# RMSNorm with every row written twice: one VectorE copy of two rows becomes two copies of one row

## The chip, the cores and the metric

The kernel runs on one core of a Trainium2 chip. The metric is the device time of one execution in microseconds (us). The kernel before took 238.42 us, the median of three runs that lie between 238.42 and 239.19 us.

The engines that matter here are ScalarE (ACT in the profile), VectorE (DVE), GpSimd (POOL), SyncE (SP, which issues the transfers of `x` and of the output), and the core's 16 DMA engines, which carry the transfers. TensorE (PE) computes nothing here.

## The reference

`x` is 8 x 512 rows of 2048 float32 numbers, `gamma` is one row of 2048. Each row is divided by its root mean square and multiplied by `gamma`, and every result row stands twice in the output, one directly after the other:

```
x_rep  = np.repeat(x, 2, axis=1)                       # (8, 1024, 2048)
rms    = np.sqrt((x_rep ** 2).mean(axis=-1, keepdims=True) + 1e-6)
out    = (x_rep / rms * gamma[None, None, :]).astype(np.float32)
```

So 33.55 MB are read and 67.11 MB are written. The work on a row is done once; the second output row is a copy.

## The kernel before, in words

**Tiling.** The 4096 rows are cut into four loads. One load (`load`, L50) brings eight consecutive rows to each of the 128 partitions: 128 x 16384 float32, 8.39 MB. Each load makes two stores (`store`, L53): four input rows of a partition, scaled and doubled, are eight output rows, again 128 x 16384 float32 and 8.39 MB. There are four loads and eight stores of the same size.

**Memory.** All of it passes through one buffer `y` in SBUF with 24 rows for each partition, named in three blocks of eight: `first` (rows 0 to 7), `second` (8 to 15), `third` (16 to 23). A load's data sit in rows 4 to 11 or in rows 16 to 23. A block of eight rows that is ready to store holds result rows at even places and their copies at odd places.

**Order.** The order is written by hand (L84 turns the automatic scheduling off), so each engine does its instructions in the order in which `four` lists them, and semaphores make one engine wait for another. `four(n, ...)` handles two loads and their four stores; it is called twice, as the two groups of the title. In one group:

1. SP issues both loads.
2. First tile (rows 4 to 7 of `y`): `squares` (ScalarE, L63, a sum of squares for each row, then the root at L67) and `scale` (VectorE, the reciprocal at L73, then for each row one multiplication by the reciprocal and by `gamma` at L75). `repeat` (L82) copies rows: two on ScalarE, two on VectorE. Store 0.
3. Second tile (rows 8 to 11 of `y`, L100 to L103): the four rows are scaled from the last to the first and spread out to rows 14, 12, 10 and 8. ScalarE then copies the two upper ones (to rows 15 and 13), VectorE the two lower ones (from 8 to 9 and from 10 to 11). Store 1 follows at L103. **The change is in VectorE's copy here.**
4. Third and fourth tile (from the second load): L104 takes the squares of both, then both are scaled and copied, and all these copies are ScalarE's. Store 2 is from block `first`, store 3 from block `third`.

**Waits around the change.** VectorE's copy at L102 stands behind the four multiplications of its tile on the same engine. Store 1 on SP waits for that copy and for ScalarE's copy at L101. VectorE's next instruction after the copy is the reciprocal of the third tile, which waits for ScalarE's root. The multiplications after it write into block `first`, so they wait until store 0 has landed. On SP, store 2 stands behind store 1 and waits for ScalarE's copies at L106 and L107. The loads of the second group stand behind store 3 and wait for stores of the first group to land, since they write over the same rows.

`gamma` is brought in once at the start, over ACT's DMA queue, and spread to all partitions by GpSimd (L131, L135).

Of the kernel before, what the change touches and what calls it, by code (L numbers as in the profile page):

```python
# [1 line left out]

# [4 lines left out]


@with_exitstack
def kernel(  # L10
    ctx: ExitStack,
    tc: tile.TileContext,
    x: bass.AP,
    gamma: bass.AP,
    out: bass.AP,
):
    nc = tc.nc
    P = nc.NUM_PARTITIONS
    f32 = mybir.dt.float32
    Act = mybir.ActivationFunctionType  # L20
    Alu = mybir.AluOpType

    B, S, D = x.shape
    Bo, So, Do = out.shape
    R = So // S
    assert R == 2 and D == Do and B == Bo and So == S * R
    eps = 1e-6
    inv_d = 1.0 / float(D)


    K = 4
    N = B * S
    ntiles = N // (P * K)
    assert N % (P * K) == 0 and ntiles == 8
    H = 2
    x_t = x.rearrange("b s d -> (b s) d").rearrange("(n p k) d -> n p k d", p=P, k=H * K)
    out_t = out.rearrange("b s d -> (b s) d").rearrange("(n p h j) d -> n h p (j d)", p=P, h=H, j=K * R)

    singles = ctx.enter_context(tc.tile_pool(name="singles", bufs=1))
    rows = ctx.enter_context(tc.tile_pool(name="rows", bufs=1))  # L40
    junk = ctx.enter_context(tc.tile_pool(name="junk", bufs=1, space=bass.MemoryType.PSUM))
    small = ctx.enter_context(tc.tile_pool(name="small", bufs=4))

    y = rows.tile([P, 3 * K * R, D], f32, name="y")
    first, second, third = 0, K * R, 2 * K * R

    def load(n, at):
        nc.sync.dma_start(out=y[:, at : at + H * K, :], in_=x_t[n])  # L50

    def store(n, h, to):
        nc.sync.dma_start(  # L53
            out=out_t[n, h], in_=y[:, to : to + K * R, :].rearrange("p j d -> p (j d)")
        )

    def squares(at, rows):

        n = len(rows)
        ss = small.tile([P, n], f32, name=f"ss{n}")  # L60
        for c, k in enumerate(rows):
            sq = junk.tile([P, D], f32, name="sq")
            nc.scalar.activation(  # L63
                out=sq[:], in_=y[:, at + k, :], func=Act.Square, accum_out=ss[:, c : c + 1]
            )
        rms = small.tile([P, n], f32, name=f"rms{n}")
        nc.scalar.activation(out=rms[:], in_=ss[:], func=Act.Sqrt, scale=inv_d, bias=eps_t[:])  # L67
        return rms

    def scale(at, to, rows, rms):  # L70
        n = len(rows)
        rstd = small.tile([P, n], f32, name=f"rstd{n}")
        nc.vector.reciprocal(out=rstd[:], in_=rms[:])  # L73
        for c, k in enumerate(rows):
            nc.vector.scalar_tensor_tensor(  # L75
                out=y[:, to + R * k, :], in0=y[:, at + k, :], scalar=rstd[:, c : c + 1],
                in1=gamma_b[:], op0=Alu.mult, op1=Alu.mult,
            )

    def repeat(to, k0, k1, copy):  # L80
        y_r = y[:, to + R * k0 : to + R * k1, :].rearrange("p (k r) d -> p k r d", r=R)
        copy(out=y_r[:, :, 1, :], in_=y_r[:, :, 0, :])  # L82

    ctx.enter_context(tc.manual_schedule())  # L84

    half = K // 2
    up, down = list(range(K)), list(range(K - 1, -1, -1))

    def four(n, constants):


        load(n, first + K)
        constants()
        load(n + 1, third)
        for rows in (up[:half], up[half:]):
            scale(first + K, first, rows, squares(first + K, rows))
        repeat(first, 0, half, nc.scalar.copy)
        repeat(first, half, K, nc.vector.tensor_copy)
        store(n, 0, first)
        scale(second, second, down, squares(second, down))  # L100
        repeat(second, half, K, nc.scalar.copy)  # L101
        repeat(second, 0, half, nc.vector.tensor_copy)  # L102
        store(n, 1, second)  # L103
        roots = [squares(third + h * K, up) for h in range(H)]  # L104
        scale(third, first, up, roots[0])
        repeat(first, 0, half, nc.scalar.copy)  # L106
        repeat(first, half, K, nc.scalar.copy)  # L107
        store(n + 1, 0, first)
        scale(third + K, third, up, roots[1])
        repeat(third, 0, K, nc.scalar.copy)  # L110
        store(n + 1, 1, third)

    gamma_b = singles.tile([P, D], f32, name="gamma_b")
    G, E = 16, 3
    C = D // G - E
    gamma_s = y[0:1, 0:2, :].rearrange("p k (c d) -> p (k c) d", c=G // 2)
    gamma_t = y[0:1, 2, :]
    eps_t = singles.tile([P, 1], f32, name="eps_t")

    def constants():  # L120
        nc.scalar.dma_start(
            out=gamma_s[0:1, :, :C],
            in_=gamma[: G * C].rearrange("(p c d) -> p c d", p=1, c=G),
        )
        for c in range(E):
            at = G * C + c * G
            nc.scalar.dma_start(
                out=gamma_t[0:1, c * G : (c + 1) * G],
                in_=gamma[at : at + G].partition_broadcast(1),
            )  # L130
        nc.gpsimd.partition_broadcast(  # L131
            out_ap=gamma_b[:, : G * C].rearrange("p (c d) -> p c d", c=G),
            in_ap=gamma_s[0:1, :, :C],
        )
        nc.gpsimd.partition_broadcast(out_ap=gamma_b[:, G * C :], in_ap=gamma_t[0:1, : E * G])  # L135
        nc.vector.memset(eps_t, eps)  # L136

        root = singles.tile([P, 1], f32, name="root")[:]
        nc.scalar.activation(out=root, in_=eps_t[:], func=Act.Sqrt)  # L139

    four(0, constants)
    four(2, lambda: None)


# [1 line left out]
_INS = ['x', 'gamma']  # L146
_OUTS = [((8, 1024, 2048), 'float32')]


# [23 lines left out]
```

## Time and profile before

| What | Before |
|---|---|
| median of three runs | 238.42 us |
| the profiled execution, its own time | 238.52 us |
| span of the profiled execution | 236.3 us |
| DVE busy | 84.4 us (36%), 47 instructions |
| ACT busy | 110.2 us (47%), 86 instructions |
| POOL busy | 2.8 us (1%) |
| packets of the transfers of `x` and the output | 98.7% of 16 engines' span |
| bytes moved | 100.68 MB, 426 GB/s over the span |
| VectorE copies of 128x4096 | 4, 2.294 us each |

The span runs from the first to the last recorded event; the execution's own time is 2.2 us longer. A busy time is the sum of an engine's instructions and says nothing on whether anyone waited for them. In a row of instruction groups, "L82 DVE COPY y<-y 128x4096" is line 82 of the kernel, engine VectorE, a copy inside the buffer `y` of 4096 elements in each of 128 partitions. In a row of the timeline, the first two numbers are the start and the duration in us, and the bracket at the end says how long the engine had been idle before it and what ended that idle time. SPq is SP's sequencer, which issues transfers.

### The profile page before, as it was taken

How to read it: one execution, taken by the hardware profiler on the slowest of the kernel's cores; microseconds unless marked ns; L12 is line 12 of the kernel's file. 1: busy time of each engine (PE TensorE's matmuls, PEld its weight loads, DVE VectorE, ACT ScalarE, POOL GpSimd, SP SyncE). 2: the span in 40 equal slices, each digit the busy share in tenths (PEclk: the TensorE clock that was granted, in tenths of full speed). 3: DMA queues.
4: the chain of work that ended last, by engine and by line, in shares of the span. 5: the costliest groups of instructions: out<-in, count | busy, mean ns of one | idle time of the engine just before them, and what ended most of it. 6: DMA issues, size and time to landing. Idle time of an engine off the chain costs nothing.

```text
span 236.3 us, 225 instructions
## 1 busy us (share of the span) xinstructions
DVE 84.4 (36%) x47; ACT 110.2 (47%) x86; POOL 2.8 (1%) x6
## 2 busy tenths in 40 slices
DVE  0000396594699500000000007929919992000000
ACT  2001989479998470000000049991999957400000
POOL 0110000000000000000000000000000000000000
DMA  9898989989898989999898988989898988989894
GB/s 355 356 532 355 521 366 466 422 388 499 355 532 356 521 366 466 422 399 488 355 532 355 510 377 377 510 355 532 355 532 355 510 377 388 499 355 532 355 532 177
DMA packets 1767, 100.68 MB, mean 426 GB/s; under 512 B 230, under 2 KB 230, under 8 KB 230
## 3 DMA queue, kind: packets, MB, share of 16 engines
q1 hardware_dynamic: 1728, 100.66, 98.7%
q10 hardware_dynamic: 38, 0.01, 0.0%
q14 instruction: 1, 0.01, 0.0%
HBM read 33.56 MB, written 67.11 MB: 426 GB/s over the span
## 4 chain that ended last, share of the span: by engine, by line
DMA 45%; ACT 26%; DVE 12%; issue 2%; DVEq 0%
DMA y<-in_x_dram 26%; DMA out_dram<-y 19%; ACT sq L63 15%; DVE y L75 12%; ACT y L82 11%; ACT rms L67 1%; DVE rstd L73 0%; DVEq L75 0%
## 5 line engine op out<-in xcount | busy, mean ns | idle before, releaser
L63 ACT ACTIVATE sq<-y 128x2048 f32<-128x2048 f32 x32 | 60.1, 1878 | 71.1 <-DMA y<-in_x_dram 70.4
L75 DVE SCALAR_TENSOR_TENSOR y<-y,rstd,gamma_b 128x2048 f32<-128x2048 f32 x32 | 73.8, 2348 | 1.6 <-DMA out_dram<-y 1.0
L82 ACT COPY y<-y 128x4096 f32<-128x4096 f32 (+1 forms) x10 | 42.6, 4283 | 19.1 <-DVE y L75 18.3
L73 DVE RECIPROCAL rstd<-rms 128x4 f32<-128x4 f32 (+1 forms) x10 | 1.7, 170 | 109.2 <-ACT rms L67 109.2
L82 DVE COPY y<-y 128x4096 f32<-128x4096 f32 x4 | 9.2, 2294 | 0.1
L63 ACT ACTIVATION_READ_ACCUMULATOR sq<-y 128x1 f32 x32 | 6.0, 186 | 0.0
L67 ACT ACTIVATE rms<-ss,eps_t 128x4 f32<-128x4 f32 (+1 forms) x10 | 3.0, 297 | 0.3
L139 ACT ACT_TABLE_LOAD x1 | 1.3, 1283 | 2.6 <-issue 2.6
L131 POOL PARTITION_BROADCAST gamma_b<-y x1 | 2.2, 2243 | 10.2 <-DMA y<-in_gamma_dram 10.2
L135 POOL PARTITION_BROADCAST gamma_b<-y x1 | 0.3, 323 | 10.2 <-DMA y<-in_gamma_dram 10.2
L136 DVE MEMSET eps_t<- 128x1 f32 x1 | 0.1, 59 | 0.8 <-PEq L157 0.8
L139 ACT ACTIVATE root<-eps_t 128x1 f32<-128x1 f32 x1 | 0.2, 202 | 0.0
L157 POOL MEMSET const-bfloat16-1.0<- 128x1 bf16 x1 | 0.1, 101 | 0.0
L157 POOL MEMSET const-uint8-127<- 128x1 uint8 x1 | 0.1, 101 | 0.0
L157 POOL MEMSET const-float32-0.0<- 128x1 f32 x1 | 0.1, 98 | 0.2 <-issue 0.2
L157 POOL MEMSET const-float32-1.0<- 128x1 f32 x1 | 0.1, 99 | 0.0
## 6 DMA issues: line engine op xcount, KB each, us to landing
out_dram<-y SPq DMA_DIRECT2D x8, 24.7
y<-in_x_dram SPq DMA_DIRECT2D x4, 31.4
y<-in_gamma_dram ACTq DMA_DIRECT2D x3, 0.1 KB
y<-in_gamma_dram ACTq DMA_DIRECT2D x1, 7.8 KB, 9.9
```

The costliest lines, as they stand in the source:

```text
L63: nc.scalar.activation(out=sq[:], in_=y[:, at + k, :], func=Act.Square, accum_out=ss[:, c : c + 1])
L67: nc.scalar.activation(out=rms[:], in_=ss[:], func=Act.Sqrt, scale=inv_d, bias=eps_t[:])
L73: nc.vector.reciprocal(out=rstd[:], in_=rms[:])
L75: nc.vector.scalar_tensor_tensor(out=y[:, to + R * k, :], in0=y[:, at + k, :], scalar=rstd[:, c : c + 1], in1=gamma_b[:], op0=Alu.mult, op ...
L82: copy(out=y_r[:, :, 1, :], in_=y_r[:, :, 0, :])
L131: nc.gpsimd.partition_broadcast(out_ap=gamma_b[:, : G * C].rearrange("p (c d) -> p c d", c=G), in_ap=gamma_s[0:1, :, :C],)
L135: nc.gpsimd.partition_broadcast(out_ap=gamma_b[:, G * C :], in_ap=gamma_t[0:1, : E * G])
L136: nc.vector.memset(eps_t, eps)
L139: nc.scalar.activation(out=root, in_=eps_t[:], func=Act.Sqrt)
L157: nc = _bacc.Bacc("TRN2", target_bir_lowering=False, num_devices=1)
```

## The change

In `four`, which runs once for each group, VectorE's copy of rows 8 and 10 of the buffer to rows 9 and 11 as one instruction of 128 x 2 x 2048 elements is written as two instructions of 128 x 2048 elements: first row 8 to 9, then row 10 to 11. Nothing else in the code changes; the lines behind it move down by one.

```
         scale(second, second, down, squares(second, down))
         repeat(second, half, K, nc.scalar.copy)
-        repeat(second, 0, half, nc.vector.tensor_copy)
+        for k in range(half):
+            repeat(second, k, k + 1, nc.vector.tensor_copy)
         store(n, 1, second)
```

Here `half` is 2 and `K` is 4.

## The prediction, made before the changed kernel ran

> **What bounds the kernel now.** I read the queues first, because the kernel does little arithmetic on each byte. The page's part on DMA queues:
>
> ```profile
> q1 hardware_dynamic: 1728, 100.66, 98.7%
> HBM read 33.56 MB, written 67.11 MB: 426 GB/s over the span
> ```
>
> Queue 1 holds the four loads and eight stores. Its packets take 98.7% of what 16 DMA engines have in the span, so hardly any time is left in which no transfer runs. VectorE (36%) and ScalarE (47%) are mostly idle.
>
> Next the chain of waits, for the moments at which transfers land:
>
> ```profile
> 0.72 21.98 DMA y<-in_x_dram
> ...
> 76.20 23.79 DMA out_dram<-y
> ...
> 100.00 38.79 DMA y<-in_x_dram
> ...
> 155.26 22.28 DMA out_dram<-y
> ```
>
> Load 0 lands at 22.70, store 2 of the first group at 99.99, the second group's first load at 138.79, its store 0 at 177.54. In their order in the queue these are transfers 1, 5, 7 and 9. So four transfers take 77.29 us (19.32 each), the next two 38.80 (19.40 each), the next two 38.75 (19.38 each). Three remain: 3 x 19.35 = 58.05 brings the last landing to 235.6, and the span ends at 236.3. The twelve transfers run end to end at one pace. Load 0 took 21.98, about 2.6 more than the pace; that is the start of an empty queue.
>
> Last I read the timeline around the copy, in both groups, with SP's issues:
>
> ```profile
> 44.26 9.26 DVE L75 SCALAR_TENSOR_TENSOR y<-y,rstd,gamma_b 128x2048 f32<-128x2048 f32 x4
> 48.91 3.60 ACT L82 COPY y<-y 128x4096 f32<-128x4096 f32 x1 [4.89 <-DVE y L75]
> 53.56 2.29 DVE L82 COPY y<-y 128x4096 f32<-128x4096 f32 x1
> 55.94 0.34 SPq L53 DMA_DIRECT2D out_dram<-y  x1
> 60.88 0.18 DVE L73 RECIPROCAL rstd<-rms 128x4 f32<-128x4 f32 x1 [5.03 <-ACT rms L67]
> 61.48 9.14 DVE L75 SCALAR_TENSOR_TENSOR y<-y,rstd,gamma_b 128x2048 f32<-128x2048 f32 x4 [0.42 <-DMA out_dram<-y]
> ...
> 169.54 2.29 DVE L82 COPY y<-y 128x4096 f32<-128x4096 f32 x1
> 171.91 0.34 SPq L53 DMA_DIRECT2D out_dram<-y  x1
> 176.86 0.18 DVE L73 RECIPROCAL rstd<-rms 128x4 f32<-128x4 f32 x1 [5.03 <-ACT rms L67]
> ```
>
> Three things are to be seen. The copy does end last before store 1: ScalarE's half ends at 48.91 + 3.60 = 52.51, VectorE's at 53.56 + 2.29 = 55.85, and SP issues 0.09 later. But the transfer ahead of it is still running: store 0, on which the multiplication at 61.48 waits, has landed by about 61.4 (22.70 + 2 x 19.35 = 61.40). So store 1 is issued 5.46 us before the queue needs it; in the second group 177.54 - 171.91 = 5.63 us. And VectorE itself idles 5.03 us after the copy, until ScalarE's root is there.
>
> **The change part by part.**
>
> *Removed:* two VectorE copies of 128x4096, one in each group, from the row
>
> ```profile
> L82 DVE COPY y<-y 128x4096 f32<-128x4096 f32 x4 | 9.2, 2294 | 0.1
> ```
>
> *Added:* four copies of 128x2048. The trace has no VectorE copy of that shape, so I bound a pair of them. From below, half of the long copy each: 2 x 1.147 = 2.294, an extra of 0. Less than that would need the step from one row to the next inside the long copy to cost something; ScalarE's copies speak against it, since four rows (7.018 us) take less than twice the time of two rows (3.599 us). The difference, 2 x 3.599 - 7.018 = 0.18, is what one more start costs on that engine. On VectorE the reciprocals of 2 and 4 elements take 162 and 175 ns on average, nearly all of it the fixed part of an instruction; behind each other, instructions overlap a little: four multiplications of 2.348 take 9.26, so they start (9.26 - 2.348) / 3 = 2.304 apart, an overlap of 0.044. I take 0.175 - 0.044 = 0.13 us more for a pair, because this row is of the same engine. The far end is that a one-row copy lost the pace of the long one (4096 elements in 2.294 us) and went at the pace of the multiplication: 2 x 2.348 = 4.70, or 2.40 more. So the extra is between 0 and 2.40 us for each group, and 0.13 is what I take.
>
> *Moved:* nothing. Put side by side, the instruction lists of the two kernels differ on VectorE alone, by the split. SP's twelve transfers keep their order and what they wait for, ScalarE's 58 instructions too. The second short copy carries no wait of its own. POOL has done its last work by 23.4 us, over 30 us ahead of the first split copy.
>
> *Added wait:* none, but store 1 now starts after the second copy: 56.07 in place of 55.94, and 172.04 in place of 171.91. Behind store 1 on SP stands store 2, issued at 76.20 after ScalarE's copies; behind the copy on VectorE stands the reciprocal, whose idle time shrinks from 5.03 to 4.90. Nobody else waits for this copy.
>
> *The cover:* store 1 must be in the queue before store 0 lands, and earlier by what a transfer needs to get going. In the stretches of the first microseconds, the load issued at 0.72 moves nothing before 1.50:
>
> ```profile
> 0.72:1.50 0.78, 0.06 (x1) 0.00 (x0) 0.00 (x0) 1.00 0.00 0
> 1.50:3.00 1.50, 0.00 (x0) 0.41 (x1) 0.00 (x0) 1.00 2.02 699
> ```
>
> So the lead is at least 0.78 us, and at most the 2.6 us that load 0 took over the pace. Even with the 2.6, the pair may grow by 5.46 - 2.6 = 2.86 us in the first group and by 3.03 in the second before the queue runs dry. The 0.13 is a twentieth of that, and the far end of 2.40 still fits. Were the cover gone, two groups would cost 2 x 0.13 = 0.26 us.
>
> *Sum:* 238.52 (the profiled execution: its span of 236.3 and 2.2 around it) + 0 = 238.5 us. That execution stands 0.10 above the median of the runs, 238.42, inside their spread of 0.77.
>
> [...]
>
> **The rivals.**
>
> *A, the extra start is exposed or something gets in between the two copies (slower).* Place: VectorE between the short copies. Price: one us of total time for each us by which a pair grows beyond the cover, 2.86 and 3.03 us by the careful reading. To be slower by 0.5% (1.2 us, which is about what a measurement of this kernel can tell from no change) the two groups must together exceed their cover by 1.2 us, that is grow by about 3.5 us each. Two copies at the multiplication's pace grow 2.40 and don't reach it. A pair that grew by 4 us would give 238.5 + 1.14 + 0.97 = 240.6. Nothing on VectorE in the trace shows a gap of this kind between instructions without a wait: the copy follows the multiplication within 0.04 us.
>
> *B, the transfers change pace (either sign).* Stretches between issues that wait on landings give the spread of one transfer: 100.00 to 119.61 is 19.61, 119.61 to 138.79 is 19.18. If all twelve went at 19.6, the time would be 12 x 0.25 = 3.0 us longer (241.5), at 19.2 it would be 1.8 us shorter (236.7). It decides from 0.1 us for each transfer on. For it: the transfers are the bound, so any change in them counts in full. Against it: those two stretches hold no VectorE and no ScalarE work at all, and they average 19.40, the same as the 19.32 and 19.38 of the stretches full of copies. A copy of the same bytes cut in two has no way to show there.
>
> *C, the copy was on the path and gets quicker (faster).* Were two short copies quicker than the long one and the path through them bare, the gain would be at most the whole copy in both groups, 2 x 2.29 = 4.6 us, to 233.9. Against it stands the queue at 98.7%: it is already full when store 1 arrives, 5.46 us early.
>
> *D, the change doesn't do what it says.* The lists of instructions show two copies of 128x2048 in place of one, in both groups, so this is out; merged again, the time would be 238.5 as well.
>
> **How the numbers follow.** No change, by the cover: 0.89. Rival A 0.02, since a pair would have to take over twice its time. Rival B 0.07, split 0.04 slower and 0.03 faster, for what a trace of one execution can't exclude. Rival C 0.02. So faster by over 0.5% is 0.05, within 0.5% is 0.89, slower 0.06. The range is that of the first case: the unknown cost of the pair adds nothing up to 2.40 us, so it rests on the spread of the runs, 0.77 us, taken about once to either side of 238.5 and a little more for rival B: 237.6 to 239.4. A wider range would only add rivals of 0.11 together.
>
> **What would show each step.** Right: four copies of 128x2048 with a mean between 1.15 and 1.3 us; VectorE idle about 4.9 us after the pair; store 1 issued near 56.1 and 172.0; queue 1 again above 98%; store 0 of the second group landing near 177.5; span near 236.3. Wrong on the copy's price: a mean near 2.35 us, with the time unchanged all the same. Wrong on the cover: a lower share of queue 1 and a gap in the transfers behind store 0. Wrong by rival B: store 1 issued in time, the queue full, and the landings still drift from the 19.35 pace.

## The result

The changed kernel took 238.20 us, the median of 21 runs (238.13 to 238.82), against 238.62 us for 21 runs of the kernel before (238.40 to 239.22). The ratio is 0.9987 with a 95% interval of 0.9981 to 0.9992. That is 0.13% faster, 0.3 to 0.4 us. It lies inside the predicted range, and inside the 0.5% that the text called no change; but the interval does not hold 1, so the predicted difference of nothing was wrong by these 0.3 us. Where they come from is the question of the experiments.

The profiled execution took 238.17 us, its span 236.2. On the page of the changed kernel, the queue of the loads and stores:

```profile
q1 hardware_dynamic: 1728, 100.66, 98.7%
```

and in its groups of instructions, kept apart by shape, VectorE's copies:

```profile
L82 DVE COPY y<-y 128x2048 f32<-128x2048 f32 x4 | 4.7, 1223 | 0.1
L82 DVE COPY y<-y 128x4096 f32<-128x4096 f32 x2 | 4.6, 2294 | 0.1
```

The queue is as full as before. A short copy takes 1.223 us, half of the long one and 0.076 more.

The timeline of the changed kernel around the pair, in both groups:

```profile
53.48 2.36 DVE L82 COPY y<-y 128x2048 f32<-128x2048 f32 x2
55.92 0.34 SPq L53 DMA_DIRECT2D out_dram<-y  x1
60.80 0.18 DVE L73 RECIPROCAL rstd<-rms 128x4 f32<-128x4 f32 x1 [4.96 <-ACT rms L67]
61.42 9.14 DVE L75 SCALAR_TENSOR_TENSOR y<-y,rstd,gamma_b 128x2048 f32<-128x2048 f32 x4 [0.44 <-DMA out_dram<-y]
...
169.54 2.36 DVE L82 COPY y<-y 128x2048 f32<-128x2048 f32 x2
171.98 0.34 SPq L53 DMA_DIRECT2D out_dram<-y  x1
176.87 0.18 DVE L73 RECIPROCAL rstd<-rms 128x4 f32<-128x4 f32 x1 [4.96 <-ACT rms L67]
```

The pair takes 2.36 us where the one copy took 2.29. Store 1 of the second group is issued at 171.98 in place of 171.91, and VectorE waits 4.96 us behind the pair where it had waited 5.03. And the chain of waits, for the landings:

```profile
0.72 21.89 DMA y<-in_x_dram
...
76.13 23.81 DMA out_dram<-y
...
99.95 38.83 DMA y<-in_x_dram
...
155.26 22.19 DMA out_dram<-y
```

Load 0 lands at 22.61, 0.09 us earlier than before; this is 30 us ahead of the first split copy. From there on the landings stand at 99.94, 138.78 and 177.45: 77.33, 38.84 and 38.67 us apart, before 77.29, 38.80 and 38.75. Nothing got faster at the place of the change.

So the profile shows no gain inside the work. It shows one elsewhere. The time of an execution is its span and a rest around it. In the two profiles the time fell by 0.35 us (238.52 to 238.17), the span by 0.13 (236.324 to 236.191), and the rest by 0.22, from 2.20 to 1.98. In all 21 runs of the changed kernel the rest is between 1.92 and 2.02, with a mean of 1.96. (The span of a run is on record to 0.1 us only, so a single rest is good to 0.05; the means are better.) It scatters far less than the span, so it is the figure to follow.

### The profile page after: what moved, and what is told of

Same layout as the page of the kernel before. It is cut to its first block, busy times and chain, and to the rows that moved or that the text cites. A ratio compares the mean times of both kernels' runs of the same rounds, so it can differ in the third digit from the quotient of the medians.

```text
span 236.2 us, 227 instructions
## 1 busy us (share of the span) xinstructions
DVE 84.6 (36%) x49; ACT 110.2 (47%) x86; POOL 2.8 (1%) x6
## 3 DMA queue, kind: packets, MB, share of 16 engines
q1 hardware_dynamic: 1728, 100.66, 98.7%
## 4 chain that ended last, share of the span: by engine, by line
DMA 45%; ACT 26%; DVE 12%; issue 2%; DVEq 0%
DMA y<-in_x_dram 26%; DMA out_dram<-y 19%; ACT sq L63 15%; DVE y L75 12%; ACT y L82 11%; ACT rms L67 1%; DVE rstd L73 0%; DVEq L75 0%
## 5 line engine op out<-in xcount | busy, mean ns | idle before, releaser
L82 DVE COPY y<-y 128x2048 f32<-128x2048 f32 (+1 forms) x6 | 9.3, 1580 | 0.1
```

## The experiments

Three theories stood against each other at first: "the split" (two short copies help by themselves), "chance" (two timings of one kernel may differ by 0.1%), and "length of the program" (two more VectorE instructions shorten the rest, whatever they do). "Around the span" in the expectations is the rest: time less span, taken for every run and averaged.

### One kernel twice, and the change once more

e1 is the kernel before, unchanged; e2 is the changed kernel.

> The kernel before, unchanged, timed as if it were a change: it shows how far two timings of one and the same kernel stand apart here. Theory 'the split' (the 0.13% comes from cutting the copy in two): a ratio of 1.000, with an interval that holds 1, within 0.05%; span about 236.3 us and about 2.2 us around it. Theory 'chance' (the 0.13% is what two timings of one kernel may differ by): a ratio that lies 0.1% or more from 1, or an interval that does not hold 1.

> The changed kernel once more. Theory 'the split': ratio about 0.9987 again, that is 0.3 us less. Theory 'chance': a ratio between 0.999 and 1.001. Both expect two short copies of 1.22 us each, store 1 issued near 56.0 and 171.9 us, and no gap in the transfers.

Measured, e1: ratio 0.9995 (0.9986 to 1.0004), rest 2.21 us over 11 runs. The 33 runs of the kernel before beside it have a rest of 2.20, between 2.15 and 2.24. Measured, e2: ratio 0.9984 (0.9971 to 0.9997), rest 1.96 over 11 runs, between 1.92 and 2.01. So the rests of the two kernels don't overlap in any run, while their spans do: 236.2 to 237.9 in the 33 runs of before, 236.2 to 236.7 in e2. Of the difference of the means (238.37 against 238.69, 0.32 us) the rest holds 0.25, and the 0.08 of the spans is small against their scatter: the spans of e1 lie 0.11 below those of the same kernel beside it. Chance falls for the rest.

### The same number of instructions, nothing split

```
         repeat(second, 0, half, nc.vector.tensor_copy)
+        nc.vector.memset(pad[:, n // 2 : n // 2 + 1], 0.0)
```

> The long copy stays in one piece, and VectorE gets two instructions more in all, one memset of 128x1 (about 59 ns) behind the copy of the second tile in each group. The program is as many instructions longer as the changed kernel, but nothing is split. Theory 'length of the program' (what gets shorter is outside the work, in the start or the end of the execution, because the program has two more VectorE instructions): ratio about 0.9987, and the time around the span falls from about 2.2 to about 2.0 us. Theory 'the split': ratio 1.000, since the copy is whole. Theory 'chance': a ratio anywhere within 0.1% of 1.

Measured: ratio 0.9992 (0.9983 to 1.0001), rest 1.96 us over 11 runs (1.92 to 2.01). The copy is whole in its timeline:

```profile
53.49 2.29 DVE L82 COPY y<-y 128x4096 f32<-128x4096 f32 x1
55.73 0.06 DVE L103 MEMSET pad<- 128x1 f32 x1
60.81 0.18 DVE L73 RECIPROCAL rstd<-rms 128x4 f32<-128x4 f32 x1 [5.02 <-ACT rms L67]
```

A memset of 0.06 us in idle time does to the rest exactly what the split does. The theory "the split" falls for this part of the gain: it isn't the copies that make the rest shorter. The whole time is 0.27 us lower in the mean, but its interval still holds 1, so here the rest shows the effect and the total alone would not.

### The split at another place

```
-        repeat(first, half, K, nc.vector.tensor_copy)
+        for k in range(half, K):
+            repeat(first, k, k + 1, nc.vector.tensor_copy)
```

> The same split, but of VectorE's copy of the first tile (ahead of store 0) in both groups; that of the second tile stays whole. The pair takes 2 x 1.22 less the overlap, about 0.07 us more than the whole copy, and store 0 is issued about 0.07 us later, near 39.3 us, 2 us before the load ahead of it has landed. Theory 'length of the program': ratio about 0.9987, as for the changed kernel. Theory 'the split': about 0.9987 only if a split helps wherever it is, else 1.000 or up to 0.14 us more. Theory 'chance': within 0.1% of 1 with no order.

Measured: ratio 0.9996 (0.9986 to 1.0005), rest 1.98 us over 11 runs (1.92 to 2.03), span 236.56 on average. Store 0 is issued at 39.23 in place of 39.24. The rest is that of the changed kernel again; the total is not separable from no change, because this kernel's spans came out 0.07 us above those of before.

### Which engine, and how many

e5 adds `nc.scalar.copy(out=pad[...], in_=eps_t[:])`, a copy of 128x1, behind ScalarE's copy in each group. e6 has the memset in the first group alone. e7 has four memsets in each group.

> Two instructions more in all, but on ScalarE: one copy of 128x1 behind its copy of the second tile in each group, about 0.2 us each. VectorE is as before. Theory 'VectorE's program' (the time around the span depends on how many instructions VectorE has): 2.20 us around the span, as before. Theory 'any longer program': 1.96 us, as in the changed kernel. Both: the span stays near 236.4 us, since the transfers are queued 4 us and more ahead.

> One VectorE instruction more: a memset of 128x1 in the first group alone. Theory 'VectorE's program, by the instruction': half the effect, about 2.08 us around the span. Theory 'VectorE's program, by a step': either 2.20 or 1.96 us, nothing between.

> Eight VectorE instructions more, four memsets of 128x1 in each group (4 x 0.06 us in idle time). Theory 'by the instruction', 0.12 us for each: 2.20 - 8 x 0.12 = 1.24 us around the span, if it goes on so far; theory 'by a step': 1.96 us again, or a value near 2.2 if the pattern returns. The span stays near 236.4 us in either case.

Measured: e5 has a rest of 2.21 us, as before; the ratio is 0.9997 (0.9982 to 1.0011). So two instructions more count on VectorE and not on ScalarE. e6, with one instruction, has a rest of 1.84 us (1.80 to 1.88) and a ratio of 0.9988 (0.9976 to 1.0001): in the rest this is more than two instructions gain, so neither "half the effect" nor "2.20 or 1.96" holds. e7 has 1.78 (1.74 to 1.81): not the 1.24 of a gain by the instruction. Its span however is 236.7 to 236.8 in all ten runs, and the total is that of before (ratio 0.9995, 0.9982 to 1.0009).

The next candidate for what orders these values is the transfer of the program itself: the page lists a queue of the kind "instruction", q14. In the kernel before and in the changed one the row says that one such transfer falls into the span. In e7 the row is

```profile
q14 instruction: 2, 0.02, 0.0%
```

The first of e7's two is the one at 75 us that every kernel here has. In the packet records behind the page there is, besides six ahead of the span, a second transfer of 8192 bytes like the first, in every kernel but e12. In e7 it starts at 191.3 us. In before it comes after the last data packet has ended, by 2.85 us, in the changed kernel by 2.32; so the page, which covers the span, doesn't count it. Its place moves with VectorE's instructions and not with ScalarE's (e5). This gave a fourth theory, "program fetch", for the runs that came after e8. That the transfer brings the next piece of VectorE's program is what the theory assumes; the records show its queue, its size and its time. "Closing" is the time from the end of the last data packet to the end of the execution, in the profiled execution of each kernel.

```
VectorE        kernel            fetch after     closing   rest, mean (runs)
instructions                     last data, us   us        us
-4             e12               none            2.95      1.78 (10)
-2             e8                3.07            3.31      2.00 (10)
 0             before            2.85            3.35      2.20 (33)
 0             e1                2.87            3.40      2.21 (11)
 0 (+2 ACT)    e5                2.88            3.40      2.21 (10)
+1             e6                2.40            3.06      1.84 (10)
+1             e9                2.34            3.01      1.84 (12)
+1             e15               2.40            3.06      1.82 (11)
+2             changed kernel    2.32            3.13      1.96 (21)
+2             e2                2.35            3.15      1.96 (11)
+2             e14               2.37            3.17      1.96 (11)
+2             e3                2.28            3.11      1.96 (11)
+2             e4                2.31            3.15      1.98 (11)
+4             e10               1.84            3.31      1.77 (4)
+4             e13               1.90            3.34      1.78 (12)
+6             e11               47 earlier      3.03      1.76 (4)
+8             e7                44 earlier      2.96      1.78 (10)
```

Where there is no fetch after the last data (e12, e11, e7), the closing takes 2.95 to 3.03 us. Where there is one, it takes up to 0.4 more. But the place of the fetch doesn't give the price: in e9 and e2 it starts 2.34 and 2.35 us after the last data, and the closings are 3.01 and 3.15. The traces show what does.

Their semaphore records go on behind the span. In every profile one semaphore, number 2, is signalled 18 times there, and the steps between these signals are the same to 0.02 us in all 17 profiles, except for two steps. The last signal lies 0.12 to 0.13 us behind the end of the execution, counted from the span's start, in all profiles but that of e8. The last column is inside the span: at the barrier that closes the kernel, where all five engines have a DRAIN, it is the time from VectorE's semaphore instruction to the start of its DRAIN, its next one.

```
VectorE        profiles                    signal    signal    VectorE's
instructions                               3 to 4    5 to 6    DRAIN, us
-4, -2, +6, +8 e12, e8, e11, e7            0.04      0.10      0.11
 0             before, e1, e5              0.04      0.51-0.53 0.11
+1             e6, e9, e15                 0.10-0.11 0.10-0.11 0.11
+2             changed, e2, e14, e3, e4    0.23-0.24 0.10      0.11
+4             e10, e13                    0.04      0.10      0.53-0.54
```

So one delay wanders through the end of the program. With four instructions more it is VectorE that comes 0.42 us late to a step inside the span. In the kernel before, a step behind the span is 0.41 us late; with two instructions more another one is 0.19 late, with one more the two together 0.07. With eight or six more, or four fewer, no step is late. In e8 the steps are those of e12, but the signals of semaphores 156 to 206, which follow in one row between the ninth and the tenth signal, start 0.38 us behind those of 54 to 155, where otherwise they start within 0.04 us of them. These delays account for the rests: 1.78 us without one, 2.20 with 0.41, 1.96 with 0.19, 1.84 with 0.07, and 1.78 again where the delay lies inside the span. In the two profiles the change moved the delay from 0.41 to 0.19 us, which is the 0.22 by which the rest fell.

The fetch isn't what the late step waits for: in every profile that has one behind the last data, it starts 0.43 to 0.70 us after that step. It follows the delay, and both move with VectorE's count. That the late engine is VectorE is seen in e10 and e13, where the DRAIN bears its name; for the steps behind the span it is argued from the count and from the like size. What VectorE does in these 0.4 us no record says, and why only 0.19 or 0.07 of them show with two or one instructions more stays open too.

### Copies left out: no fetch, and no copy

e8 drops VectorE's copy of the second tile, e12 those of both tiles.

> VectorE's copy of the second tile is left out in both groups (so rows 9 and 11 of the buffer hold no copy and the output lacks these rows); VectorE has two instructions fewer. It shows at one time what the whole copy is worth and how the length of VectorE's program counts. The prediction's view that the copy is hidden by the transfers: span near 236.4 us, store 1 issued over 2 us earlier and the transfers no sooner done; rival C (copy on the path): up to 4.6 us less. Theory 'by the instruction': about 2.44 us around the span; theory 'by a step': 2.20 us.

> All of VectorE's copies are left out (of both tiles and both groups, so the output lacks these rows): four VectorE instructions fewer than before. Theory 'program fetch': the fetch comes later still after the span's end, near 2.0 to 2.1 us (1.69 before, 1.89 with two fewer), or not at all; the time around the span then goes towards the 1.78 us that was seen with no fetch there. The span stays near 236.3 us, since the transfers are the same. Theory 'the copies bound the kernel': several us less.

Measured, e8: span 236.2 to 236.6, ratio 0.9993 (0.9983 to 1.0002), rest between 1.81 and 2.16 with a mean of 2.00. Neither of the two numbers expected of the rest was met. The timeline of e8:

```profile
53.71 0.34 SPq L53 DMA_DIRECT2D out_dram<-y  x1
60.98 0.18 DVE L73 RECIPROCAL rstd<-rms 128x4 f32<-128x4 f32 x1 [7.36 <-ACT rms L67]
61.58 2.35 DVE L75 SCALAR_TENSOR_TENSOR y<-y,rstd,gamma_b 128x2048 f32<-128x2048 f32 x1 [0.42 <-DMA out_dram<-y]
```

Store 1 is issued 2.23 us earlier (53.71 against 55.94), and store 0, ahead of it in the queue, has landed no sooner: VectorE still waits for it until 61.58. The span is 0.12 us shorter on average than that of the kernel before, which is inside the scatter. So the whole copy is worth 0.1 us at most. This settles rival C of the prediction, which had up to 4.6 us.

Measured, e12: no fetch after the span at all, and a rest of 1.78 us, as the theory "program fetch" had it (the number; what is waited for is another thing, as said above). But the span is 237.63 us on average, 1.1 us more than before, and the ratio is 1.0024 (1.0008 to 1.0040). Nobody expected that. Leaving out the first tile's copy brings store 0's issue from 39.24 to 37.00, while the load ahead of it is still running, and that load's packets then take 2.56 us on average in place of 2.42. The loss sits in the 16 packets of it that start between 38 and 40 us, 3.56 us each in the mean. Its last data, and all that follows, come 1.5 us later in the profile, 1.1 on average over the runs. That the earlier issue is the cause was not tried and stays open: in e8 store 1 is issued as much earlier, behind another store, and that store's packets take 2.42 us as before; in the second group of e12, where store 0 is issued about 5 us ahead of its load's last data, the load's packets take 2.43.

### How much cover there was

```
-        repeat(second, 0, half, nc.vector.tensor_copy)
+        for _ in range(3):
+            repeat(second, 0, half, nc.vector.tensor_copy)
```

e10 copies three times in each group, e11 four times.

> VectorE does its copy of the second tile three times in each group, so store 1 is issued about 4.6 to 4.8 us later, near 60.6 and 176.6 us, with 0.8 to 0.9 us left before the transfer ahead of it lands. The prediction gave the lead that a transfer needs as between 0.78 and 2.6 us: with 0.78 the span stays near 236.4 us, with 2.6 it grows by about 1.7 us in each group, to near 239.8. Without any cover it would grow by 9 us.

> The same copy four times in each group: store 1 is issued about 6.9 to 7.1 us later, near 62.9 and 178.9 us, about 1.5 us after the transfer ahead of it has landed. The cover of the prediction is then used up: the span grows by 1.5 us and the lead of 0.78 to 2.6 us in each group, 4.5 to 8.2 us in all. Were the copy not ahead of any transfer that matters, the span would stay near 236.4 us.

Measured, e10: 1.0081 (1.0051 to 1.0111), span 239.1 on average. e11: 1.0284 (1.0256 to 1.0312), span 243.95. In the stretches of e10, where the columns are the stretch, its length, then DVE, ACT, POOL, clock, DMA share and GB/s, and a packet counts where it starts:

```profile
60.00:61.00 1.00, 0.63 (x1) 0.97 (x4) 0.00 (x0) 1.00 0.01 0
61.00:62.00 1.00, 0.53 (x2) 1.00 (x1) 0.00 (x0) 1.00 2.46 1049
62.00:63.00 1.00, 1.00 (x1) 0.97 (x3) 0.00 (x0) 1.00 0.00 0
```

The same stretches of the kernel before:

```profile
60.00:61.00 1.00, 0.12 (x1) 0.97 (x4) 0.00 (x0) 1.00 2.43 1049
61.00:62.00 1.00, 0.58 (x2) 1.00 (x1) 0.00 (x0) 1.00 0.00 0
62.00:63.00 1.00, 1.00 (x1) 0.97 (x3) 0.00 (x0) 1.00 0.91 393
```

In before, the first packets of store 1 start between 60 and 61 us, when the last ones of store 0 end. In e10 store 1 is issued at 60.71, and its packets start between 61 and 62: the 16 engines stood still for about a microsecond. The issue and the gap in e11:

```profile
62.75 0.34 SPq L53 DMA_DIRECT2D out_dram<-y  x1
62.79 4.61 DVE L75 SCALAR_TENSOR_TENSOR y<-y,rstd,gamma_b 128x2048 f32<-128x2048 f32 x2
```

By the packet records the first packet follows the issue by 0.84 us in both kernels, and the step from transfer 3 to transfer 4 (the mean of their packets) grew to 20.4 us in e10 and 22.4 in e11, from 19.3. So e10, which issues 0.8 us before the landing that VectorE waits for (61.64 less some 0.1), still lost 1.1 us in the first group; e11, which issues 1.2 us after it, lost 3.1. The lead that store 1 needed before the landing ahead of it is therefore about 1.9 us here, inside the prediction's 0.78 to 2.6. The cover before was 5.46 - 1.9, about 3.6 us a group; the change used 0.07 of it.

### Fewer splits, more splits

e9 and e15 are the same kernel, which splits the copy in the first group alone. e13 splits all four of VectorE's long copies. e14 is the changed kernel beside them.

```
-        repeat(second, 0, half, nc.vector.tensor_copy)
+        step = 1 if n == 0 else half
+        for k in range(0, half, step):
+            repeat(second, k, k + step, nc.vector.tensor_copy)
```

> The split of the change in the first group alone: VectorE has one instruction more than before, and a useful one. Theory 'program fetch' (the 8 KB transfer that brings the next piece of VectorE's program comes after the span, and its place there follows from the number of VectorE's instructions): as with one memset more, the fetch about 1.19 us after the span's end and 1.84 us around the span, so about 238.1 us, less than the changed kernel. Theory 'the split': half the gain, about 2.08 us around the span and a time between the two kernels.

> All four of VectorE's long copies are split, those of the first tile too: four VectorE instructions more than before, all of them useful. Theory 'program fetch': as with four instructions more in the kernel that copies three times, the fetch starts about 0.3 us after the span's end, 1.77 us are left around the span, and the span stays at 236.4 us on average, so the time is 0.43 us below before and 0.2 us below the changed kernel. Theory 'each split gains': twice the gain of the changed kernel, 0.5 to 0.6 us, and in the span. Theory 'store 0 becomes late' (its issue moves by 0.07 us): the span grows by no more than 0.07 us in each group.

> The changed kernel beside the other two on the same chip: 1.96 us around the span by the theory 'program fetch', 0.24 us below before; the theory 'each split gains' expects the same total but not where it lies.

> The split in the first group alone, beside the other two: theory 'program fetch' 1.84 us around the span, 0.12 us less than the changed kernel, though it has fewer splits; theory 'each split gains': 0.12 us more than the changed kernel.

Measured: e9 0.9978 (0.9963 to 0.9993), rest 1.84. On one chip e15 0.9977 (0.9967 to 0.9987) with a rest of 1.82, e14 0.9980 (0.9970 to 0.9990) with 1.96, e13 1.0001 (0.9987 to 1.0015) with 1.78. One split gains more in the rest than two, by 0.14 us, and four gain nothing in the total: the reverse of "each split gains". The medians of e15 and e14 are 238.11 and 238.18 us; in the whole time the two can't be told apart.

e13 met the expected rest and missed the expected total, because its span is 236.6 us or more in all 12 runs. Its profile shows why. The waits of SP's queue, in e13:

```profile
SPq L170 <- DMA out_dram<-y: 31.6, 2, 19.2
SPq L170 <- PEq L170: 0.9, 2, 0.8
```

and in the changed kernel:

```profile
SPq L169 <- DMA out_dram<-y: 31.6, 2, 19.3
SPq L169 <- PEq L169: 0.6, 2, 0.4
```

The last column is the longest wait. At the barrier that closes the kernel, SP waits 0.8 us in e13 and 0.4 in the changed kernel. The view names PE's sequencer as the releaser, but the instructions of that barrier show that VectorE comes last, in e13:

```profile
L170 SPq DRAIN  x3: 7/7/7, 235.5 to 235.8; - x3
L170 DVEq DRAIN  x2: 125/1255/2385, 193.9 to 236.3; - x2
```

and in the changed kernel:

```profile
L169 SPq DRAIN  x3: 7/7/7, 235.4 to 235.7; - x3
L169 DVEq DRAIN  x2: 19/1203/2387, 193.8 to 235.8; - x2
```

The time behind "to" is the start of the last one. In the changed kernel VectorE (DVEq) comes to this point with SP, in e13 about half a microsecond after it. The fetch of e13 starts only at 236.97 us, 0.34 after the span's end, so it can't be what SP waits for here. So the 0.4 us went from the rest into the span, and the closing as a whole is 3.34 us, about that of before (3.35). e10 has the same wait and a closing of 3.31. What counts is the closing, not the rest alone; the expectation for e13 had taken the span's share of it as fixed.

The fetch inside the work that every kernel has costs nothing that shows: in the kernel before it starts at 74.9 us and moves 8192 bytes in 0.31 us, and the transfers keep their steps of 19.3 us across it. At the end of the kernel a delay of 0.4 us comes ahead of a fetch; whether the two belong together, no run here shows.

## Why the prediction was right or wrong

- **The bound: right.** The queue of the loads and stores is at 98.7% before and after, and the landings keep their distances.
- **The price of the pair: right in kind, too high.** Predicted 0.13 us more, in bounds of 0 to 2.40; measured 0.07 (2.36 against 2.29). The short copy kept the pace of the long one. The mean of 1.223 lies in the announced 1.15 to 1.3.
- **Hidden by store 0: right.** Store 1 was issued 0.07 us later in the second group. Taking the copy away brought at most 0.1 us to the span (e8), and adding 4.6 us and more to it cost 2.5 and 7.4 us of span (e10, e11). The cover exists and it is finite.
- **The lead: right within its bounds**, about 1.9 us between 0.78 and 2.6. The 2.86 us given for the cover "by the careful reading" was about 0.7 too small.
- **The sum: wrong by 0.3 us.** The step that failed is "238.52 (the profiled execution: its span of 236.3 and 2.2 around it) + 0". It took the 2.2 around the span as a constant. They are 1.96 to 1.98 in each of the kernels with two more VectorE instructions, copies or memsets, because a delay in the closing that holds up a step by 0.41 us in the kernel before shows as 0.19 there. On the path, the two instructions more were taken as worth nothing because their cover by store 0 holds; it holds, and what they changed lies behind the last transfer. The rivals looked for a mechanism inside the work, at the copy, the queue and the pace; none of them had the closing of the kernel.
- **Rival A:** out; the pair grew by 0.07 us, not by over 3. **Rival B:** out as a cause; the distances of the landings moved by 0.08 us at most, of either sign. **Rival C:** out by e8. **Rival D:** out by the profile's four short copies.
- **Within 0.5%: right**, and so was the range. The gain of 0.13% became visible only by 21 runs on each side.

## What to carry to other kernels

Where the transfers are queued ahead of the engine, as here, the cost of an edit on it is judged by the lead of the next issue over the landing ahead of it (5.46 us, of which about 1.9 were needed), not by the share of busy time (36%). A gain of 0.1% that shows up with no mechanism inside the work should be split into span and rest first: a dummy instruction of 0.06 us told the two apart here. And this gain went with the number of VectorE's instructions (a rest of 2.20 us before, 1.84 with one more, 1.96 with two), so the next edit on the same engine may take it back, as the four splits did (ratio 1.0001).

## What was not expected of the hardware

- A delay of about 0.4 us at the end of the kernel, which shows at VectorE's DRAIN in e10 and e13 (0.53 to 0.54 us in place of 0.11) and is VectorE's elsewhere by argument only, moves the time by up to 0.4 us, not in proportion to the instructions added: the closing is 3.35 to 3.40 us, then 3.01 to 3.06 with one VectorE instruction more, 3.11 to 3.17 with two, 3.31 to 3.34 with four, 2.96 with eight. In every profile with an 8192-byte instruction transfer behind the last data, that transfer starts 0.43 to 0.70 us after the late step; with eight there is none.
- With eight instructions more the fetch falls into the work, at 191.3 us, and the span grew to 236.7 to 236.8 us in every run. It takes 0.31 us while the queue is full; that this accounts for the growth is the author's estimate and was not tried by itself.
- With a store issued 2.2 us earlier behind a load still running, 16 packets of that load took 3.56 us each in the mean, where its packets take 2.42 in the kernel before, and the work ended 1.1 us later on average (e12). The cause is open.
